# A hybrid decoder in split float32: modulation sums finished as columns, rotary products merged, evictions moved within their step

## The chip, the cores and the metric

The kernel runs on one core of one Trainium2 chip. The metric is the device time of one execution in microseconds (us); the kernel before takes 1912.27 us, the median of three runs (1906.89 to 1913.08). The engines are named as in the profile: PE (TensorE, matmuls), PEld (its weight loads), DVE (VectorE), ACT (ScalarE), POOL (GpSimd) and SP (SyncE, which here issues nearly all DMAs). Each engine works through its own instructions in a fixed order and waits at an instruction whose inputs, or whose buffer, aren't ready.

## The reference

Two layers are applied to 1024 positions of width 1024. Each has a token-mixing and a channel-mixing sub-layer, both normalised, both modulated by a vector `c`:

```python
mod = silu(c) @ ada_w[l] + ada_b[l]              # 6 x 1024
shift_m, scale_m, gate_m, shift_f, scale_f, gate_f = split(mod, 6)
h = rms_norm(x, g_pre_mix[l]) * (1 + scale_m) + shift_m
q, k, v, u = split(h @ w_in[l] + b_in[l])
q, k = partial_rotary(q), partial_rotary(k)      # first 16 of each head's 64
mix = concat(window_attention(q, k, v, sinks[l]), causal_pool(u)) @ w_out[l]
x = x + gate_m * rms_norm(mix, g_post_mix[l])
h = rms_norm(x, g_pre_ffn[l]) * (1 + scale_f) + shift_f
f = (silu(h @ w_gate[l]) * (h @ w_up[l])) @ w_down[l]
x = x + gate_f * rms_norm(f, g_post_ffn[l])
```

There are 8 query heads and 2 key heads, a window of 128, and an FFN of width 2816. All in float32.

## The kernel before

**Matmuls.** A float32 product is made of three matmuls on halves. `split` (L218) rounds a tile into a high part by a cast on ACT (L220) and takes the rest as a low part by a subtraction on DVE (L221); `mm3` (L262) issues high x high, low x high and high x low (L263, L266, L267) into one accumulator bank `acc`. Four such banks hold the four 128-row tiles of half the sequence (512 positions, `T`); each half is carried by itself. `msc` are banks for transposes and small products.

**Order.** The program is written as generators that yield at their steps. `run` (L682) advances a main stream and, by given ratios, side streams beside it; the instructions go into a scheduler that lays out each engine's order. So what is written ahead of a `yield`, or behind it, decides beside which main step it stands.

**A layer's stages.** `dense` (L1461) holds the projection of the pooled channels (`u_pass`, L754) and of queries and keys (`q_pass`, `kv_pass`), with attention on the first half beside it. `mix_out` (L1011) is the output projection, done by `natural_proj` (L653) in two halves of 512 columns (`nh`); for each, eight steps `k` add into the four banks, and behind the last one the banks are read: the squares' sum on ACT (`square_sum`, L501) and a product with the gate row `G` on DVE (L680). Attention on the second half runs beside it: `att_rotary` (L776) turns queries and keys in six DVE operations of 128x80 (L784 to L789), `att_keys` and `att_queries` split (L809, L832) and transpose them (L814, L835), the scores follow (L855, L856), then the softmax (L858 to L883) and its transposes (L893). The FFN's up products come in pairs of column blocks (`up_pair`, L1126): sums of weight blocks on DVE (L1166, L1167, L1171, L1172), each then split and multiplied in a product of 24 matmuls (T2, T3, T1, B22, T4), the banks combined on DVE (L1151). L1172 makes the operand of T3. The down products follow.

**The modulation** is a side stream. One sum (`ada_sum`, L285) covers 512 of the 6144 outputs: eight slices of `ada_w`, 128x512 each, are loaded into `ar` (two buffers) and added on DVE into one tile `ada`, scaled by `c` (L296 the first, L298 the rest). This leaves 128 partial sums a column, still to be added over the partitions. Three ways follow. For the FFN's shift and scale (`ada_pair`, L404) and for the gates (`ada_gate`, L457) the tile is split into two `ph` tiles and two matmuls with a picking vector `picks` add over the partitions to a row (L412, L413; L469, L470). `ada_pair` then gathers four rows and transposes them to columns (L420). A gate stays a row: bias and weight are loaded as rows into `ar` (L466, L467) and applied in two DVE operations of 1x512 (L471, L472), and the row is written to memory (L473), from where `load_gate` (L482) spreads it over the partitions as `G`. For the next layer's token-mixing (`ada_columns`, L435) four matmuls take 128 columns of `ada` each as weights and a column of ones as the moving operand, so the sums come out as columns at once (L441). `ada_stream` (L487) runs the sums one after another and closes each right behind its last step.

## Time and profile before

| | |
|---|---|
| median of 3 runs | 1912.27 us |
| the profiled execution's own time | 1915.26 us |
| its span | 1913.5 us |
| mean granted PE clock | 0.993 |
| busy: PE / DVE / ACT | 98% / 81% / 49% of the span |
| L298, the accumulations of the modulation | 140 times, 746 ns each, 104.5 us busy |
| L220 / L221, the splits | 388 times each, 868 / 986 ns |

The time runs slightly past the span, which begins with the first instruction that the profile shows. Start times in rows are from the span's start. The mean durations of L220 and L221 mix tiles of 128x512 and of 128x1024. In a row of a timeline "x4" stands for neighbouring instructions that were put together, and the bracket gives how long the engine was idle ahead of the row and whose end it waited for. The first layer takes about the first half of the span, the second the rest: its stages come some 940 us later.

### The profile page before, as it was taken

What the parts mean: (1) busy time and instruction counts of PE and PEld (TensorE: products, weight loads), DVE (VectorE), ACT (ScalarE), POOL (GpSimd) and SP (SyncE); (2) the same over time, 40 slices, a digit from 0 to 9 for tenths busy, and PEclk for the clock granted to TensorE, in tenths of its full rate; (3) what the DMA queues carried; (4) which work ended last, traced back from release to release, by engine and by line L of the source; (5) the groups of instructions that cost most, each with busy time, mean ns of one, the idle gap of its engine ahead of it and who ended that gap; (6) DMA issues with size and microseconds to landing.
All of it is one profiled execution on the core that took longest, in us unless ns stands there. A gap on an engine that the chain in (4) does not pass through costs nothing.

```text
span 1913.5 us, 26037 instructions
## 1 busy us (share of the span) xinstructions
PE 1866.0 (98%) x8954; PEld 1541.1 (81%) x8954; DVE 1541.9 (81%) x2913; ACT 946.4 (49%) x1786; POOL 20.4 (1%) x67
## 2 busy tenths in 40 slices
PE   7999999999999999999999989999999999999997
PEld 5887788888878788888888868888887887888886
DVE  7899886678788888788878988846888888877687
ACT  4875795553222223445548667845622222244452
POOL 0000000000000000000000000000000000000000
PEclk9999999999999999999999989999999999999999
DMA  9345563555555655944554464536754566574342
GB/s 343 108 144 161 160 220 127 187 182 192 183 180 187 206 206 172 320 144 149 175 175 138 125 179 165 177 110 211 218 181 149 197 211 201 198 251 150 114 152 102
DMA packets 229540, 341.86 MB, mean 179 GB/s; under 512 B 17016, under 2 KB 126472, under 8 KB 229408
## 3 DMA queue, kind: packets, MB, share of 16 engines
q1 hardware_dynamic: 228800, 338.10, 53.6%
q10 hardware_dynamic: 576, 2.10, 0.3%
q8 instruction: 70, 1.15, 0.2%
q14 instruction: 62, 0.51, 0.1%
q0 software_dynamic: 32, 0.00, 0.0%
HBM read 267.25 MB, written 72.89 MB: 178 GB/s over the span
## 4 chain that ended last, share of the span: by engine, by line
PE 77%; DVE 12%; DMA 5%; ACT 3%; issue 2%; SPq 0%; DVEq 0%; ACTq 0%; POOL 0%; POOLq 0%
PE acc L263 24%; PE acc L266 23%; PE acc L267 23%; DMA ar<-in_ada_w_dram 2%; DVE lo L221 2%; DMA raw<-in_w_up_dram 2%; DVE ada L298 1%; PE msc L893 1%; PE msc L561 1%; ACT hi L220 1%; DVE fn L1151 1%; PE pv L263 1%; PE pv L266 1%; ACT raw L554 1%; DMA ar<-x 1%
## 5 line engine op out<-in xcount | busy, mean ns | idle before, releaser
L220 ACT ACTIVATE hi<-raw 128x1024 fp32r<-128x1024 f32 (+1 forms) x388 | 331.9, 868 | 364.9 <-PE acc L266 198.8
L221 DVE TENSOR_TENSOR lo<-raw,hi 128x1024 fp32r<-128x1024 f32 (+1 forms) x388 | 379.9, 986 | 121.6 <-ACT hi L220 117.4
L263 PE MATMUL acc<-t,hi 128*128 128x512 f32 x704 | 275.1, 391 | 5.8 <-ACT hi L220 5.8
L266 PE MATMUL acc<-t,hi 128*128 128x512 f32 x704 | 274.7, 390 | 0.0
L267 PE MATMUL acc<-t,lo 128*128 128x512 f32 x704 | 272.1, 390 | 0.1
L263 PE MATMUL acc<-bh,hi 128*128 128x512 f32 x520 | 202.9, 390 | 0.0
L267 PE MATMUL acc<-bh,lo 128*128 128x512 f32 x520 | 202.4, 389 | 0.0
L263 PE MATMUL acc<-hT,hi 128*128 128x512 f32 x480 | 190.2, 396 | 0.6 <-DVE fn L680 0.6
L266 PE MATMUL acc<-hT,hi 128*128 128x512 f32 x480 | 188.4, 393 | 0.0
L267 PE MATMUL acc<-hT,lo 128*128 128x512 f32 x480 | 187.5, 391 | 0.0
L1151 DVE TENSOR_TENSOR fn<-acc,fn 128x512 f32<-128x512 f32 x220 | 150.3, 684 | 39.4 <-PE acc L267 39.1
L263 PEld LDWEIGHTS acc<-t,hi 128*128 128x128 f32 x704 | 132.4, 188 | 35.3 <-ACT hi L220 8.2
L267 PEld LDWEIGHTS acc<-t,lo 128*128 128x128 f32 x704 | 132.4, 188 | 29.3 <-DVE lo L221 1.5
L266 PEld LDWEIGHTS acc<-t,hi 128*128 128x128 f32 x704 | 132.5, 188 | 27.2
L266 PE MATMUL acc<-ph,hi 128*128 128x512 f32 x320 | 124.7, 390 | 0.0
L1087 ACT ACTIVATE fn<-fn 128x512 f32<-128x512 f32 x44 | 27.8, 633 | 185.7 <-DVE fn L1151 185.7
L298 DVE SCALAR_TENSOR_TENSOR ada<-ar,c_act,ada 128x512 f32<-128x512 f32 x140 | 104.5, 746 | 12.5 <-DMA ar<-in_ada_w_dram 11.3
L267 PEld LDWEIGHTS acc<-bh,lo 128*128 128x128 f32 x520 | 97.6, 188 | 20.4
L263 PEld LDWEIGHTS acc<-bh,hi 128*128 128x128 f32 x520 | 97.6, 188 | 20.2 <-ACT sb L1249 0.2
L263 PE MATMUL acc<-hi 128*128 128x512 f32 x256 | 103.6, 410 | 2.4 <-DVE fn L680 2.0
L263 PEld LDWEIGHTS acc<-hT,hi 128*128 128x128 f32 x480 | 90.2, 188 | 19.2 <-DVE fn L680 1.4
L267 PEld LDWEIGHTS acc<-hT,lo 128*128 128x128 f32 x480 | 90.1, 188 | 18.6 <-issue 0.2
(315 smaller groups left out, 3813.5 us busy)
## 6 DMA issues: line engine op xcount, KB each, us to landing
ar<-in_ada_w_dram SPq DMA_DIRECT2D x160, 256.0 KB
raw<-in_w_gate_dram SPq DMA_DIRECT2D x44, 512.0 KB
raw<-in_w_up_dram SPq DMA_DIRECT2D x44, 512.0 KB
raw<-in_w_in_dram SPq DMA_DIRECT2D x80, 256.0 KB
raw<-keeps SPq DMA_DIRECT2D x40, 512.0 KB
keeps<-fn SPq DMA_DIRECT2D x66, 256.0 KB
two_b<-in_w_down_dram SPq DMA_DIRECT2D x30, 512.0 KB
raw<-keepa SPq DMA_DIRECT2D x25, 512.0 KB
```

Source lines behind the costliest of these rows:

```text
L220: a = nc.scalar.activation(hi, src, AF.Copy)
L221: v = nc.vector.tensor_sub(lo, src, hi.bitcast(F32))
L263: ins = nc.tensor.matmul(dst, lh, rh, start=first, stop=False)
L266: nc.tensor.matmul(dst, lh, rl, start=False, stop=False)
L267: return nc.tensor.matmul(dst, ll, rh, start=False, stop=last)
L298: ins = nc.vector.scalar_tensor_tensor(acc, w, c_act[:, i : i + 1], acc, op0=ALU.mult, op1=ALU.add)
L554: nc.scalar.activation(hf, bank, AF.Identity, bias=shift, scale=scale)
L561: ins = nc.tensor.transpose(bank[:, t * P : (t + 1) * P], src[t], ident)
L893: nc.tensor.transpose(bank[:, i * P : (i + 1) * P], s[:, ii, ck * P : (ck + 1) * P], ident)
L1087: nc.scalar.activation(g, g, AF.Silu)
L1151: nc.vector.tensor_add(halves_of(dst)[m], bank, halves_of(src)[m])
```

## The change

**Sums as columns.** All sums now finish as `ada_columns` does: a helper `column_sums` issues the four matmuls with `ada` as weights. `ada_pair` is gone, and `ada_columns` serves the FFN's shift and scale. A gate is handled as a column too: bias and weight come from the transposed table `cols` (16 rows longer, from two more short loads a layer), two DVE operations of 128x4 replace those of 1x512, and the column is written to memory in elements of 4 bytes. The splits into `ph` and `picks` are gone for these sums.

**One step later.** `ada_stream` closes a sum only behind the first step of the next one.

**Rotary.** The tables of cosine and sine are doubled along a new axis, so that two products of 128x160 and two combinations of 128x80 replace the six operations; `vz` has four buffers instead of five.

**Evictions.** `natural_proj` reads each bank right behind its own last matmul, inside the last step, and `u_pass` its banks ahead of its last yield.

The core of the diff:

```diff
-    def ada_sum(l, n0, got, whole=False):
+    def ada_sum(l, n0, got):
...
-        if whole:
-            got.append(acc)
-        else:
-            got += [t_("ph", [P, 512], F32R), t_("ph", [P, 512], F32R)]
-            split(*got, acc)
+        got.append(acc)
         yield
...
+    def column_sums(acc):
+        bank = msc_bank()
+        for i in range(4):
+            nc.tensor.matmul(
+                bank[:, i : i + 1], acc[:, i * P : (i + 1) * P], ones[:, 0:1], start=True, stop=True
+            )
+        return bank[:, 0:4]
...
-        def close(half, hi, lo):
...
-            nc.sync.dma_start(gb, ada_b[l : l + 1, n0 : n0 + 512])
-            nc.sync.dma_start(gg, (g_post_ffn if sub else g_post_mix)[l : l + 1, o])
-            bank = msc_bank()
-            nc.tensor.matmul(bank[0:1, :], picks[:, 3:4], hi, start=True, stop=False)
-            nc.tensor.matmul(bank[0:1, :], picks[:, 3:4], lo, start=False, stop=True)
-            nc.vector.tensor_add(gb, bank[0:1, :], gb)
-            nc.vector.tensor_mul(gb, gb, gg)
-            nc.sync.dma_start(row[:, o], gb)
+        def close(half, acc):
+            bank = column_sums(acc)
...
+            nc.vector.tensor_add(gc, bank, cols[:, k0 : k0 + 4])
+            nc.vector.tensor_mul(gc, gc, cols[:, g0 : g0 + 4])
+            nc.sync.dma_start(row[0, half * 512 : half * 512 + 512].rearrange("(i p) -> p i", p=P), gc)
...
-        for l, n0, close, *whole in jobs:
+        ending = None
+        for l, n0, close in jobs:
             got = []
-            yield from ada_sum(l, n0, got, *whole)
-            close(*got)
+            for i, _ in enumerate(ada_sum(l, n0, got)):
+                yield
+                if ending and i == 0:
+                    ending()
+            ending = lambda close=close, got=got: close(*got)
+        yield
+        if ending:
+            ending()
...
                     mm3(banks[t], lh[:, tiles[t]], ll[:, tiles[t]], wh, wl, k == 0, k == K - 1)
+                    if k == K - 1:
+                        square_sum(ss, t, nh, banks[t])
+                        nc.vector.tensor_mul(fn[t][:, cs], banks[t], G[:, cs])
                 yield
-            for t in range(NT):
-                square_sum(ss, t, nh, banks[t])
-                nc.vector.tensor_mul(fn[t][:, cs], banks[t], G[:, cs])
...
-            yield
+            if k < KD - 1:
+                yield
         for g in range(4):
             ut = t_("uT", [P, UW])[:, : HALO + T]
...
             uts.append(ut)
+        yield
...
-        tmp = t_("rt", [P, 4, nr, RH])
-        nc.vector.tensor_mul(tmp[:, 0], t1, cb)
-        nc.vector.tensor_mul(tmp[:, 1], t2, sbc)
-        nc.vector.tensor_mul(tmp[:, 2], t2, cb)
-        nc.vector.tensor_mul(tmp[:, 3], t1, sbc)
-        nc.vector.tensor_sub(t1, tmp[:, 0], tmp[:, 1])
-        nc.vector.tensor_add(t2, tmp[:, 2], tmp[:, 3])
+        tmp = t_("rt", [P, 2, nr, ROT])
+        nc.vector.tensor_mul(tmp[:, 0], rot, cb)
+        nc.vector.tensor_mul(tmp[:, 1], rot, sbc)
+        for i in range(2):
+            a, b = slice(i * RH, (i + 1) * RH), slice((1 - i) * RH, (2 - i) * RH)
+            nc.vector.tensor_tensor(
+                out=rot[:, :, a], in0=tmp[:, 0, :, a], in1=tmp[:, 1, :, b], op=ALU.subtract if i == 0 else ALU.add
+            )
```

Three places in the engines' orders, before and after. The changed program has line numbers of its own: its L261, L264 and L265 are `mm3`, L788 and L809 the transposes of keys and queries (before L814, L835), L403 the column sum, L296 the accumulation (before L298), L650 the eviction (before L680).

The first is the border from `dense` to `mix_out` in the first layer, at 162 us of the trace. PE's order before:

```order
L267 MATMUL acc<-hi,uT 128x512
L412 MATMUL msc<-ph,picks 4x512
L413 MATMUL msc<-ph,picks 4x512
L814 MATMUL msc<-ident,hi 128x128 x4
L263 MATMUL acc<-hi 128x512 x3
L835 MATMUL msc<-ident,hi 128x128 x4
```

PE's order there in the changed kernel:

```order
L265 MATMUL acc<-hi,uT 128x512
L403 MATMUL msc<-ones_r,ada 128x1 x4
L788 MATMUL msc<-ident,hi 128x128 x4
L809 MATMUL msc<-ident,hi 128x128 x4
L261 MATMUL acc<-hi 128x512 x4
```

DVE's order at the same place in the changed kernel (`colp` are the finished columns, L757, L758 and L761 the rotary, L783 and L806 the splits that were L809 and L832):

```order
L296 SCALAR_TENSOR_TENSOR ada<-ar,c_act,ada 128x512
L758 TENSOR_TENSOR rt<-qkv,sin_t 128x160
L296 SCALAR_TENSOR_TENSOR ada<-ar,c_act,ada 128x512
L761 TENSOR_TENSOR qkv<-rt 128x10x8 x2
L415 TENSOR_TENSOR colp<-msc,cols 128x4
L775 TENSOR_TENSOR vz<-qkv,vz 128x64
L395 SCALAR_TENSOR_TENSOR colp<-colp,cols 128x4
L775 TENSOR_TENSOR vz<-qkv,vz 128x64
L757 TENSOR_TENSOR rt<-qkv,cos_t 128x160
L783 TENSOR_TENSOR hi<-qkv,hi 128x2x128
```

The column sum stands where the two picks stood, directly ahead of the keys' transposes, and on DVE the addition that reads it (L415) stands ahead of the split that those transposes read (L783).

The second is the border between the halves of `mix_out` in the second layer, at 1134 us. DVE's order before:

```order
L221 TENSOR_TENSOR ph<-msc,pth 128x512
L298 SCALAR_TENSOR_TENSOR ada<-ar,c_act,ada 128x512
L832 TENSOR_TENSOR hi<-qkv,hi 128x4x64
L680 TENSOR_TENSOR fn<-acc,G 128x512 x2
L298 SCALAR_TENSOR_TENSOR ada<-ar,c_act,ada 128x512
L680 TENSOR_TENSOR fn<-acc,G 128x512
L298 SCALAR_TENSOR_TENSOR ada<-ar,c_act,ada 128x512
L680 TENSOR_TENSOR fn<-acc,G 128x512
```

DVE's order there in the changed kernel (L832 is the softmax's masked maximum, L219 a split):

```order
L296 SCALAR_TENSOR_TENSOR ada<-ar,c_act,ada 128x512
L650 TENSOR_TENSOR fn<-acc,G 128x512
L415 TENSOR_TENSOR colp<-msc,cols 128x4
L650 TENSOR_TENSOR fn<-acc,G 128x512
L294 TENSOR_SCALAR ada<-ar,c_act 128x512
L832 ISA sb,st<-msc,mask 128x256
L832 ISA st 128x1
L832 ISA sb,st<-msc,mask 128x256
L832 ISA st 128x1
L219 TENSOR_TENSOR ph<-msc,pth 128x512
L296 SCALAR_TENSOR_TENSOR ada<-ar,c_act,ada 128x512
L650 TENSOR_TENSOR fn<-acc,G 128x512 x2
```

The first two evictions have moved ahead of the first accumulation of a new sum, the maxima and the split; the last two now stand behind them.

The third is the fifth pair of the FFN's products in the first layer, at 645 us. DVE's order before:

```order
L1088 TENSOR_TENSOR fn<-fn 128x512
L1172 TENSOR_TENSOR raw<-raw 128x8x128
L1196 TENSOR_TENSOR fn<-fn 128x512
L1151 TENSOR_TENSOR fn<-acc,fn 128x512
L221 TENSOR_TENSOR ph<-ada,ph 128x512
```

DVE's order there in the changed kernel (L1062, L1125, L1146 and L1170 are the former L1088, L1151, L1172 and L1196; `gc` is the gate's column):

```order
L1062 TENSOR_TENSOR fn<-fn 128x512
L1125 TENSOR_TENSOR fn<-acc,fn 128x512
L1170 TENSOR_TENSOR fn<-fn 128x512
L1146 TENSOR_TENSOR raw<-raw 128x8x128
L1125 TENSOR_TENSOR fn<-acc,fn 128x512
L435 TENSOR_TENSOR gc<-msc,cols 128x4
L436 TENSOR_TENSOR gc<-gc,cols 128x4
```

The sum of weight blocks (L1146) has gone behind an addition from the banks and a difference, and the gate's column comes out directly behind.

More of the change, by code (lines that the diff above doesn't have):

```diff
@@ L96, in hybrid_decoder_kernel @@
     dr = ctx.enter_context(tc.tile_pool(name="dr", bufs=1, space=DRAM))
-    SMALL = dict(junk=1, st=12, rs=8, ss=4, halo=8, rows=1, cols=2, colp=4, sk=2)
+    SMALL = dict(junk=1, gc=3, st=12, rs=8, ss=4, halo=8, rows=1, cols=2, colp=4, sk=2)
     SHARED = dict(hT=8, fn=4, raw=2, hi=3, lo=3, sa=2, sb=2, ar=2, ada=1, ph=3, G=1)
     REGIONS = dict(
-        mix=dict(cfa=2, cfb=2, qkv=5, bqkv=1, uT=4, pt=2, vz=5, rt=1, qT=1, pth=2, pwh=1, pwl=1),
+        mix=dict(cfa=2, cfb=2, qkv=5, bqkv=1, uT=4, pt=2, vz=4, rt=1, qT=1, pth=2, pwh=1, pwl=1),
         up=dict(t2=8, t1=8, t3=8, b22=8, t4=8),
@@ L147, in hybrid_decoder_kernel @@
     ones_r = const.tile([P, 1], F32R, name="ones_r")
-    picks = const.tile([P, 7], F32R, name="picks")
     c_raw = const.tile([P, KD], F32, name="c_raw")
@@ L450, in ada_columns @@
         return [
-            (l, (3 * sub + 1 - r // 2) * D + r % 2 * 512, lambda acc, r=r: close(r, acc), True)
+            (l, (3 * sub + 1 - r // 2) * D + r % 2 * 512, lambda acc, r=r: close(r, acc))
             for r in range(4)
```

79 lines of the change are left out of this document (23 added, 56 removed).

## Prediction

> **What bounds the kernel now.** I read the page's busy times first, then the waits of PE, then PE's rows around each long wait, and last the granted clock in windows of 3 us.
>
> ```profile
> PE 1866.0 (98%) x8954; PEld 1541.1 (81%) x8954; DVE 1541.9 (81%) x2913; ACT 946.4 (49%) x1786; POOL 20.4 (1%) x67
> ```
>
> ```profile
> PE msc L332 <- DVE ident L152: 11.1, 1, 11.1
> PE acc L263 <- ACT hi L220: 6.1, 5, 2.1
> PE msc L893 <- DVE sb L883: 3.8, 7, 0.9
> ```
>
> PE is the bound: work added to it costs its full length unless it falls into a wait, and work taken from another engine pays only where PE waits for it. The waits that the change can reach lie in the two mix stages. PE's timeline (start, duration, idle before it in brackets, and who ended the idle):
>
> ```profile
> 164.04 0.39 PE L412 MATMUL msc<-ph,picks 128*4 128x512 f32 x1 [1.76 <-ACT ph L220]
> 164.85 0.59 PE L413 MATMUL msc<-ph,picks 128*4 128x512 f32 x1 [0.43 <-DVE ph L221]
> 165.28 0.72 PE L814 MATMUL msc<-ident,hi 128*128 128x128 f32 x4
> ...
> 194.54 0.53 PE L835 MATMUL msc<-ident,hi 128*128 128x128 f32 x4 [1.41 <-DVE fn L680]
> ...
> 196.41 0.79 PE L263 MATMUL acc<-hi 128*128 128x512 f32 x1 [0.47 <-DVE fn L680]
> ...
> 1104.77 0.51 PE L814 MATMUL msc<-ident,hi 128*128 128x128 f32 x4 [1.67 <-DVE rt L787]
> 1105.55 0.97 PE L263 MATMUL acc<-hi 128*128 128x512 f32 x3 [0.27 <-ACT hi L220]
> ...
> 1134.75 0.51 PE L835 MATMUL msc<-ident,hi 128*128 128x128 f32 x4 [0.59 <-DVE hi L832]
> ...
> 1137.11 0.49 PE L263 MATMUL acc<-hi 128*128 128x512 f32 x1 [0.76 <-DVE fn L680]
> 1138.42 0.79 PE L263 MATMUL acc<-hi 128*128 128x512 f32 x1 [0.81 <-DVE fn L680]
> ```
>
> Idle: 2.19 us at 162, 1.88 at 193, 1.94 at 1103, 2.16 at 1134. Behind each the clock falls (columns: length, then busy us of PE, PEld, DVE, ACT, POOL, then the granted clock):
>
> ```profile
> 165.00:168.00 3.00, 3.00 (x13) 2.33 (x12) 3.00 (x11) 2.29 (x6) 0.00 (x0) 0.50 0.47 145
> 195.00:198.00 3.00, 2.53 (x9) 1.74 (x9) 3.00 (x6) 2.48 (x6) 0.00 (x0) 0.58 0.32 92
> ...
> 1107.00:1110.00 3.00, 3.00 (x9) 2.46 (x9) 2.96 (x5) 2.03 (x4) 0.00 (x0) 0.50 0.52 160
> ...
> 1137.00:1140.00 3.00, 2.08 (x4) 1.30 (x5) 2.84 (x8) 0.60 (x2) 0.00 (x0) 0.59 0.64 172
> 1140.00:1143.00 3.00, 3.00 (x8) 2.31 (x7) 2.95 (x11) 1.85 (x8) 0.14 (x1) 0.50 0.51 118
> 1475.00:1478.00 3.00, 1.79 (x8) 1.05 (x7) 3.00 (x5) 2.06 (x3) 0.00 (x0) 1.00 0.73 244
> ```
>
> At half clock for about 3.4 us PE loses about 1.7 us (twice that at 1137, where the low stretch covers most of two windows). A wait of 1.21 us (the 1475 window: 3.00 less 1.79 busy) left the clock at 1.00, so I take about 1.5 us idle within 3 us as the point where a fall begins. Idle and falls together cost 3.9, 3.6, 3.6 and 5.6 us at the four places: 16.7 us is all that is to be had there.
>
> The Trainium skill, "TensorE: Matmul & The Clock Gate", Part 1, puts the fall behind an idle window of about 3.4 us. No wait quoted here is that long, yet the rows show 0.50: the measurement decides. By that rule the falls would be no consequence of these waits and would stay when the waits shrink; the sum below would lose its two clock terms (4.3 us) and come out about 1916, inside the range of the forecast itself.
>
> **The change part by part.** *PE.* A sum that is a column already (L441) and a pair of picks (L469, L470):
>
> ```profile
> 790.69 0.95 PE L441 MATMUL msc<-ones_r,ada 128*128 128x1 f32 x8
> 791.50 0.49 PE L263 MATMUL acc<-bh,hi 128*128 128x512 f32 x1
> ...
> 649.88 0.40 PE L469 MATMUL msc<-ph,picks 128*1 128x512 f32 x1
> ...
> 650.35 0.43 PE L267 MATMUL acc<-t,lo 128*128 128x512 f32 x1
> ...
> 1150.05 0.41 PE L420 MATMUL msc<-ident,ar 4*128 4x4 f32 x4
> 1150.39 0.38 PE L855 MATMUL msc<-sa,qT 128*128 128x256 f32 x1
> ```
>
> Start to next start, a column sum holds PE for 0.81 us, a pair for 0.47: 16 x 0.34 = +5.4 us. The two groups of row transposes (L420, 0.34 each) go: -0.7. Four of the new sums (at 162, 197 and one in each layer's products) stand where PE waits anyway, -1.4. Net **+3.3**.
>
> *DVE and ACT.* Each of the 16 sums loses a cast and a subtraction of 128x512; the gates also swap two 1x512 operations for two of 128x4; the rotary goes from six operations to four. That is relief on an engine beside PE, worth only what it takes from PE's waits. I take **-1.0** of the waits for the softmax (L893, 3.8 us) and its like; bounds 0 and -3.8.
>
> *The border at 162.* DVE's rows:
>
> ```profile
> 162.57 0.75 DVE L298 SCALAR_TENSOR_TENSOR ada<-ar,c_act,ada 128x512 f32<-128x512 f32 x1 [0.36 <-DMA ar<-in_ada_w_dram]
> ...
> 164.72 0.42 DVE L809 TENSOR_TENSOR hi<-qkv,hi 128x256 fp32r<-128x256 f32 x1
> ```
>
> The column sum needs this L298 alone, which itself waited for its load: PE can start it at 163.3 instead of 164.04, and ends it at about 164.1. But the four transposes behind it need L809, and in the new order DVE waits for the column sum first (the addition to the columns), then has two copies, the scaling and a rotary product before L809: about 0.1 + 0.1 + 0.1 + 0.1 + 0.2 + 0.4 us from their rows' likes, so PE goes on at about 165.3, as before. The wait is cut in two, and so is what is gained: **0** (bounds -3.9 and +1).
>
> *The border at 193.* The four evictions (L680) move ahead of L809 and L832, but two L298 still stand among them, and PE now runs six attention matmuls and the first four of the next half before the transposes. By DVE's order the fourth bank comes free about 3 us after the last matmul, and the transposes wait for L809 and L832 behind it. **0** (bounds -3.6 and +2).
>
> *1103.* DVE's chain from the last of L738 to L809 is shorter by two rotary operations a block, some 0.4 us of the 1.67; the fall behind it goes with even odds. **-1.2** (bounds 0 and -3.6).
>
> *1134.* Here the evictions start before the stage's last matmuls end, and PE has eight transposes, six attention matmuls and four scores (some 2 us by the likes of their rows) before it asks for the third and fourth bank. Between the second and the third eviction, though, DVE has a sum, the softmax's maxima and a split:
>
> ```profile
> 1137.68 0.68 DVE L680 TENSOR_TENSOR fn<-acc,G 128x512 f32<-128x512 f32 x1
> ```
>
> The last eviction then ends some 3 us after the last matmul (an estimate: two evictions, the sum and a split of about 0.6 to 0.7 us each are left by then), and PE wants it at 2.5 to 3. I leave 1.0 us of idle, drop the fall, and round down: **-4.0** (bounds 0 and -5.6).
>
> *The FFN's products.* In each layer the two gate sums close one product step later. The third pair of column blocks then has on DVE, ahead of L1171 and L1172, the split of the gate slice, the gate's two small operations, L296 and one L298; in the fifth pair L1172 drops behind an eviction and L1196.
>
> ```profile
> 579.40 1.22 DVE L1166 TENSOR_TENSOR raw<-raw 128x1024 f32<-128x1024 f32 x1
> ...
> 588.27 1.21 DVE L1172 TENSOR_TENSOR raw<-raw 128x1024 f32<-128x1024 f32 x1
> ...
> 645.47 1.22 DVE L1172 TENSOR_TENSOR raw<-raw 128x1024 f32<-128x1024 f32 x1
> ```
>
> ```profile
> 646.38 0.39 PE L267 MATMUL acc<-t,lo 128*128 128x512 f32 x1
> 647.91 0.50 PE L263 MATMUL acc<-t,hi 128*128 128x512 f32 x1 [1.14 <-ACT hi L220]
> ```
>
> PE's product T3 waits for L1172 and the cast behind it. In the third pair L1172 ends at 589.48, and T3 begins (ten products of 24 steps of 0.227 us back from 646.77) at 592.2: with a cast of 1.1 us that leaves 1.6 us. The chain from L1166 to L1172 grows from 10.1 to about 13 us, but L1166 may start 1.4 us earlier, one place up: 0 to 1.4 us late. In the fifth pair 1.2 us comes on top of 1.14, of which the column sum fills 0.8. I take +0.8 a layer, **+1.6**; bounds 0 and +12.2 (below).
>
> *Queues and start.* The gate now goes out as 512 elements of 4 bytes, with the load of G right behind it on SP, and behind that the next weights:
>
> ```profile
> 1.27 5.45 DMA pos_i<-in_positions_dram
> ...
> 129.74 1.44 DMA gate<-ar
> ```
>
> ```profile
> 651.82 1.17 SPq L1134 DMA_DIRECT2D raw<-in_w_up_dram  x1
> ```
>
> ```profile
> 663.46 1.23 DVE L1166 TENSOR_TENSOR raw<-raw 128x1024 f32<-128x1024 f32 x1 [0.38 <-DMA raw<-in_w_up_dram]
> ```
>
> The row write took 1.44 us, the 4-byte read of the positions 5.45. These weights are issued 11.6 us before their first use, so up to some 4 us more of SP waiting is hidden: 0. The Trainium skill, "DMA: Bandwidth & Descriptors", Specifications, wants 512 B or more in a transfer, since shorter ones read, modify and write; it speaks against this write, and no run here shows such a write's price.
>
> ```profile
> 10.41 0.24 DVE cos_t L205
> ```
>
> At the start PE waits 11.1 us for the identity's cast behind these table operations; two rows more of them (0.2 each) and two short loads ahead of the first weights: **+0.5**, bounds 0 and +1.2.
>
> Sum: 3.3 - 1.0 + 0 + 0 - 1.2 - 4.0 + 1.6 + 0.5 = **-0.8 us** on the profiled execution's own 1915.26 us: 1914.5. That execution is 3.0 us above the median of the runs, so the forecast is **1911.5 us**.
>
> **The rivals.** *All four places empty* (DVE's relief puts it ahead everywhere): -16.7 for the -5.2 above, so 1911.5 - 11.5 = **1900 us**. For it: DVE is behind PE in each of the waits. Against: at 162 and 193 it waits for loads or has other work in front. *Slower: L1172 late in the products.* At the third pair 1.5 us of idle and a fall (3.2 us), at the fifth 1.2 us more and a fall (2.9), in two layers: 12.2 in place of 1.6, so about **1922 us**. It decides when L1172 in the third pair ends after 591.1 by today's times. For it: the same place in the first pair, with two L298 in front, shows PE's longest mid-run wait, 2.1 us. Against: DVE has slack ahead of L1166. *The change doesn't do what it says*: the evictions come early in the order but wait all the same, no mix wait shrinks, and the column sums' work stays: 3.3 + 1.6 + 0.5 = +5.4, so **1917.7 us**.
>
> **How the numbers follow.** A measurement of this kernel tells about 0.3% (5.7 us) from no change. Forecast 0.40 (1906 to 1917), all places empty 0.30, products late 0.16, only the added work 0.14, half of that beyond the bound. Faster 0.30, the same 0.47, slower 0.23. The range runs from the empty places (1899) to just below the full price of the late products (1921).
>
> **What would show it.** The columns' matmuls at 0.8 us a sum; PE's wait at 1134 under 1.2 us and the clock at 1.00 behind it; two waits instead of one at 162; PE's wait for ACT's cast in the third pair of products, absent today, under 1 us. I am wrong if the waits at 162 or 193 go (faster), or if the clock falls in the products where it does not today (slower).

## The result, and the profile after

The changed kernel takes **1942.62 us** (median of four, 1941.62 to 1946.39) against 1910.18 us of the kernel before in the same session (1906.89 to 1913.08): a ratio of 1.0174, interval 1.0150 to 1.0198. It is 32 us slower, beyond the range. The ratios here and below leave out two executions that were far slower than all others for a reason that isn't known, one of `e3_extra_small_writes` (2827 us) and one of the kernel before (6607 us).

The page of the changed kernel: busy times, and the line on DMA packets.

```profile
PE 1876.2 (97%) x9042; PEld 1556.2 (80%) x9042; DVE 1525.1 (79%) x2872; ACT 935.1 (48%) x1768; POOL 18.9 (1%) x67
...
DMA packets 233782, 341.86 MB, mean 176 GB/s; under 512 B 21249, under 2 KB 130737, under 8 KB 233649
```

The same line on packets of the kernel before:

```profile
DMA packets 229540, 341.86 MB, mean 179 GB/s; under 512 B 17016, under 2 KB 126472, under 8 KB 229408
```

DVE and ACT got the relief they were meant to get (1525 against 1542 us, 935 against 946). PE is busy 10.2 us longer, and the span of 1939.8 us leaves it idle for 63.6 us, where it was 47.5 before. There are 4,242 packets more, nearly all under 512 B: eight gate writes of 512 elements are 4,096 of them.

The waits of PE in the changed kernel (instruction, releaser: us in total, times, longest):

```profile
PE msc L867 <- DVE sb L857: 13.3, 7, 6.5
PE msc L327 <- DVE ident L151: 11.1, 1, 11.1
PE acc L261 <- ACT hi L218: 6.8, 5, 2.0
PE msc L867 <- DVE st L832: 4.4, 1, 4.4
```

The transposes of the softmax (L867, formerly L893) wait 17.7 us, where it was 3.8. What they wait for is DVE, and this is what DVE waits for, in the changed kernel:

```profile
DVE ada L296 <- DMA ar<-in_ada_w_dram: 32.0, 24, 6.4
DVE raw L1140 <- DMA raw<-in_w_up_dram: 25.6, 13, 6.6
```

and in the kernel before:

```profile
DVE raw L1166 <- DMA raw<-in_w_up_dram: 11.5, 7, 2.7
DVE ada L298 <- DMA ar<-in_ada_w_dram: 11.3, 18, 1.3
```

Loads that moved as many bytes as ever came late. The longest wait of PE shows why. SP's timeline of the changed kernel, in the mix of the second layer:

```profile
1080.04 0.68 SPq L437 DMA_DIRECT2D gate<-gc  x1
1080.83 0.45 SPq L304 DMA_DIRECT2D ar<-in_ada_w_dram  x1
...
1090.07 0.33 SPq L446 DMA_DIRECT2D G<-gate  x1
```

DVE's timeline there:

```profile
1083.91 0.70 DVE L965 TENSOR_TENSOR pt<-uT 128x527 f32<-128x527 f32 x1
1091.06 0.75 DVE L296 SCALAR_TENSOR_TENSOR ada<-ar,c_act,ada 128x512 f32<-128x512 f32 x1 [6.45 <-DMA ar<-in_ada_w_dram]
```

PE's timeline there:

```profile
1086.16 0.39 PE L261 MATMUL acc<-hi,hT 128*128 128x512 f32 x1
1093.05 0.45 PE L867 MATMUL msc<-ident,sb 128*128 128x128 f32 x1 [6.50 <-DVE sb L857]
```

And the windows (length, busy us of PE, PEld, DVE, ACT, POOL, then the granted clock, the share of time in which the DMA engines had work, and GB/s):

```profile
1082.00:1090.00 8.00, 4.54 (x25) 3.63 (x23) 2.54 (x6) 3.82 (x13) 0.00 (x0) 1.00 0.41 36
1090.00:1093.00 3.00, 0.00 (x0) 0.00 (x0) 1.94 (x9) 0.51 (x1) 0.00 (x0) 0.52 0.72 191
1093.00:1096.00 3.00, 2.95 (x9) 2.48 (x10) 2.01 (x5) 1.15 (x2) 0.00 (x0) 0.50 1.02 370
```

Read together: the gate (`gate<-gc`) goes out at 1080.04. For the next eight microseconds all DMA of the core moves 36 GB/s; then it recovers. The load of G, which needs the written gate, is issued only 10.0 us after it. The load of `ar` that SP issued 0.8 us behind the gate arrives when the gate is done, DVE stands 6.45 us before the one instruction that needs it, and the softmax, which needs nothing of it, stands behind that instruction in DVE's order. PE runs out of work for 6.50 us, and then runs at half clock. The other gates of the mix do the same: PE waits 3.81 us at 111.9 and 4.37 us at 1050.5. Not every new wait is theirs, though. One of 2.00 us in the products of the first layer, with a fall behind it, ends while the gate written at 652.97 has hardly left; it is taken up below:

```profile
653.30 0.79 PE L261 MATMUL acc<-t,hi 128*128 128x512 f32 x1 [2.00 <-ACT hi L218]
```

```profile
654.00:657.00 3.00, 3.00 (x9) 2.34 (x8) 2.78 (x3) 1.14 (x2) 0.00 (x0) 0.56 0.22 41
```

The places that the change was aimed at did improve. PE's rows of the changed kernel at the former 162, 193, 1103 and 1134:

```profile
169.81 0.51 PE L788 MATMUL msc<-ident,hi 128*128 128x128 f32 x4 [1.27 <-DVE hi L783]
...
196.98 1.15 PE L261 MATMUL acc<-hi 128*128 128x512 f32 x3 [0.72 <-ACT hi L640]
198.89 0.52 PE L261 MATMUL acc<-hi 128*128 128x512 f32 x1 [0.76 <-DVE fn L650]
...
1127.34 0.51 PE L788 MATMUL msc<-ident,hi 128*128 128x128 f32 x4 [1.37 <-DVE hi L783]
...
1157.05 0.38 PE L829 MATMUL msc<-sa,qT 128*128 128x256 f32 x1 [0.55 <-ACT qT L814]
...
1160.18 0.50 PE L264 MATMUL acc<-lo,hi 128*128 128x512 f32 x1 [1.06 <-DVE lo L219]
```

The windows behind them:

```profile
168.00:171.00 3.00, 1.73 (x15) 1.53 (x16) 2.41 (x12) 2.18 (x6) 0.00 (x0) 1.00 0.46 152
1129.00:1132.00 3.00, 3.00 (x17) 2.55 (x16) 3.00 (x6) 3.00 (x7) 0.00 (x0) 1.00 0.49 112
1162.00:1165.00 3.00, 3.00 (x15) 2.49 (x14) 2.87 (x10) 2.44 (x9) 0.32 (x1) 1.00 0.56 169
...
201.00:204.00 3.00, 3.00 (x12) 2.74 (x12) 1.88 (x7) 2.37 (x7) 0.00 (x0) 0.50 0.36 90
```

Three of the four falls of the clock are gone in this execution; the one at 193 is still there. The experiments say what that was worth.

### The profile page after: what moved, and what is told of

It reads as the page before. It is cut to its first block, busy times and chain, and to the rows that moved or that the text cites. A ratio compares the mean times of both kernels' runs of the same rounds, so it can differ in the third digit from the quotient of the medians.

```text
span 1939.8 us, 26118 instructions
## 1 busy us (share of the span) xinstructions
PE 1876.2 (97%) x9042; PEld 1556.2 (80%) x9042; DVE 1525.1 (79%) x2872; ACT 935.1 (48%) x1768; POOL 18.9 (1%) x67
## 4 chain that ended last, share of the span: by engine, by line
PE 72%; DVE 13%; DMA 9%; ACT 4%; issue 2%; SPq 0%; DVEq 0%; ACTq 0%; POOL 0%; POOLq 0%
PE acc L261 22%; PE acc L265 22%; PE acc L264 22%; DMA raw<-in_w_up_dram 4%; DMA ar<-in_ada_w_dram 3%; DVE lo L219 2%; PE msc L867 1%; DVE fn L1125 1%; ACT hi L218 1%; DVE ada L296 1%; DMA ar<-x 1%; PE msc L532 1%; PE msc L403 1%; PE pv L261 1%; PE pv L264 1%
## 5 line engine op out<-in xcount | busy, mean ns | idle before, releaser
L219 DVE TENSOR_TENSOR lo<-raw,hi 128x1024 fp32r<-128x1024 f32 (+1 forms) x388 | 380.4, 986 | 120.6 <-ACT hi L218 118.3
L261 PE MATMUL acc<-t,hi 128*128 128x512 f32 x704 | 277.1, 394 | 6.9 <-ACT hi L218 6.8
L265 PE MATMUL acc<-t,lo 128*128 128x512 f32 x704 | 274.4, 393 | 3.3 <-DVE lo L219 3.1
L264 PE MATMUL acc<-t,hi 128*128 128x512 f32 x704 | 275.9, 392 | 0.0
L261 PE MATMUL acc<-bh,hi 128*128 128x512 f32 x520 | 202.9, 390 | 0.0
L265 PE MATMUL acc<-bh,lo 128*128 128x512 f32 x520 | 202.5, 389 | 0.0
L261 PE MATMUL acc<-hT,hi 128*128 128x512 f32 x480 | 190.7, 397 | 2.6 <-ACT uT L738 2.0
L264 PE MATMUL acc<-hT,hi 128*128 128x512 f32 x480 | 188.2, 392 | 0.0
L265 PE MATMUL acc<-hT,lo 128*128 128x512 f32 x480 | 187.8, 392 | 0.0
L1125 DVE TENSOR_TENSOR fn<-acc,fn 128x512 f32<-128x512 f32 x220 | 150.2, 683 | 40.5 <-PE acc L265 40.4
L261 PEld LDWEIGHTS acc<-t,hi 128*128 128x128 f32 x704 | 133.4, 190 | 36.5 <-ACT hi L218 9.4
L265 PEld LDWEIGHTS acc<-t,lo 128*128 128x128 f32 x704 | 133.0, 189 | 33.3 <-DVE lo L219 5.5
L264 PEld LDWEIGHTS acc<-t,hi 128*128 128x128 f32 x704 | 133.4, 189 | 27.7
L296 DVE SCALAR_TENSOR_TENSOR ada<-ar,c_act,ada 128x512 f32<-128x512 f32 x140 | 104.5, 747 | 32.8 <-DMA ar<-in_ada_w_dram 32.0
L264 PE MATMUL acc<-ph,hi 128*128 128x512 f32 x320 | 124.7, 390 | 0.0
L265 PEld LDWEIGHTS acc<-bh,lo 128*128 128x128 f32 x520 | 97.6, 188 | 20.3
L261 PEld LDWEIGHTS acc<-bh,hi 128*128 128x128 f32 x520 | 97.7, 188 | 20.0
L261 PEld LDWEIGHTS acc<-hT,hi 128*128 128x128 f32 x480 | 90.4, 188 | 21.0 <-ACT uT L738 2.4
L265 PEld LDWEIGHTS acc<-hT,lo 128*128 128x128 f32 x480 | 90.1, 188 | 18.5
L264 PEld LDWEIGHTS acc<-hT,hi 128*128 128x128 f32 x480 | 90.4, 188 | 16.4
```

The lines of the kernel that those rows point to most:

```text
L219: v = nc.vector.tensor_sub(lo, src, hi.bitcast(F32))
L261: ins = nc.tensor.matmul(dst, lh, rh, start=first, stop=False)
L264: nc.tensor.matmul(dst, lh, rl, start=False, stop=False)
L265: return nc.tensor.matmul(dst, ll, rh, start=False, stop=last)
L296: ins = nc.vector.scalar_tensor_tensor(acc, w, c_act[:, i : i + 1], acc, op0=ALU.mult, op1=ALU.add)
L1125: nc.vector.tensor_add(halves_of(dst)[m], bank, halves_of(src)[m])
```

## The experiments

Every kernel below was timed against the kernel before on the same chip; the medians of that one were between 1908.6 and 1910.2 us. A ratio stands with its 95% interval.

### Is it the gate, and which part of it?

The changed kernel with the gate turned back into a row on PE and written as a row (`e1_row_write`):

```diff
-            nc.sync.dma_start(row[0, half * 512 : half * 512 + 512].rearrange("(i p) -> p i", p=P), gc)
+            turned = msc_bank()
+            nc.tensor.transpose(turned[0:4, 0:P], gc, ident)
+            gr = t_("rows", [P, P])[0:4]
+            nc.vector.tensor_copy(gr, turned[0:4, 0:P])
+            nc.sync.dma_start(row[0, half * 512 : half * 512 + 512].rearrange("(i p) -> i p", p=P), gr)
```

> The changed kernel, but each gate column (128x4) is turned to 4x128 by a PE transpose and copied by DVE, so that it is written in four pieces of 512 B instead of 512 elements of 4 B. Theory S (the small writes clog the memory side for some 10 us, the next load for the modulation lands late, DVE waits for it and PE behind DVE): the three waits of 3.8, 4.4 and 6.5 us go, with the clock falls behind them; 1905 to 1916 us. Theory O (the loss is the order: sums closed a step later, accumulations ahead of the softmax on DVE): 1935 to 1946 us. Theory Q (the loads only stand behind the small writes in SP's own queue): as S.

The changed kernel with the gate closed as before, by a split and picks, and the other sums as columns (`e2_old_gate`):

```diff
-            bank = column_sums(acc)
...
+            split(hi, lo, acc)
...
+            nc.tensor.matmul(bank[0:1, :], picks[:, 3:4], hi, start=True, stop=False)
+            nc.tensor.matmul(bank[0:1, :], picks[:, 3:4], lo, start=False, stop=True)
...
+            nc.sync.dma_start(row[:, o], gb)
```

> The changed kernel with the gates finished as before (split, two picks, a row of 1x512, a write in one piece of 2 KB), still one step later; the FFN's shift and scale stay columns. Theory S: 1905 to 1916 us, near e1_row_write. Theory O: 1930 us or more, since order and late close stay. Theory Q: as S.

The kernel before, with a second write of 512 elements of 4 bytes beside each gate's (`e3_extra_small_writes`):

```diff
             nc.sync.dma_start(row[:, o], gb)
+            extra = dr.tile([1, 512], F32, tag="extra", name="extra", bufs=4 * DEPTH)
+            nc.sync.dma_start(extra[0].rearrange("(i p) -> p i", p=P), c_act[:, 0:4])
```

> The kernel before, with one extra write of 512 elements of 4 B (a constant tile of 128x4, to memory that nobody reads) behind each of the eight gate writes. Theory S: slower by 15 to 30 us (1925 to 1940). Theory O: within 3 us of before. Theory Q: as S, since the loads stand behind the extra writes in the same queue.

The changed kernel with the gate on ACT's queue (`e4_other_queue`):

```diff
-            nc.sync.dma_start(row[0, half * 512 : half * 512 + 512].rearrange("(i p) -> p i", p=P), gc)
+            nc.scalar.dma_start(row[0, half * 512 : half * 512 + 512].rearrange("(i p) -> p i", p=P), gc)
```

> The changed kernel, with the gate's small writes issued by ACT on its own queue instead of SP's. Theory S: the loads are as late as in the changed kernel, 1935 to 1946 us. Theory Q: the loads no longer stand behind the writes, 1908 to 1920 us. Theory O: 1935 to 1946 us.

| kernel | median us | ratio to before |
|---|---|---|
| changed | 1942.62 | 1.0174 (1.0150 to 1.0198) |
| e1_row_write | 1917.22 | 1.0045 (1.0027 to 1.0064) |
| e2_old_gate | 1921.09 | 1.0052 (1.0032 to 1.0071) |
| e3_extra_small_writes | 1931.66 | 1.0113 (1.0087 to 1.0139) |
| e4_other_queue | 1947.11 | 1.0197 (1.0178 to 1.0216) |

e1 does all that the change does, and a transposition more for each gate, and only its write is another: 25.4 us of the 32 are gone. (DVE's order changes a little with it; `e16_gate_in_16_bytes` below is free of that.) e2, whose gates are closed as before, loses 21.5 of the 32. Both stay above the 1905 to 1916 us that were expected: some 7 to 11 us of the loss have another cause. The waits of DVE for the same two loads fall as well; in e1:

```profile
DVE ada L296 <- DMA ar<-in_ada_w_dram: 17.4, 18, 2.7
...
DVE raw L1144 <- DMA raw<-in_w_up_dram: 13.1, 11, 2.3
```

The window of e1 behind the gate that cost most above, and that of e4:

```profile
1070.00:1078.00 8.00, 7.60 (x47) 6.41 (x45) 6.01 (x18) 5.48 (x14) 0.00 (x0) 1.00 0.88 277
```

```profile
1085.00:1093.00 8.00, 4.86 (x26) 3.85 (x25) 2.60 (x8) 3.58 (x13) 0.00 (x0) 1.00 0.55 82
```

e4 says that it isn't SP's queue that holds the later loads up: from another queue the write costs as much. So the theory of a queue's order falls, and what is slow is the write and, with it, all other transfers.

e3 missed its place. Its extra writes read data that is ready at the start, so the scheduler sent all eight off between 57.9 and 73 us, instead of one beside each gate. It still shows the loss, and plainly: apart from the extra writes, every engine runs the same instructions in the same order as in the kernel before. DVE waits there for a short load, and PE behind it waits 16.6 us at one transposition, where it was 0.6:

```profile
DVE sk L1354 <- DMA sk<-in_sinks_dram: 15.9, 1, 15.9
```

### What of the write is it?

The kernel before with extra writes that copy the finished gate row, so that each must stay where the gate is written. They go to memory that nobody reads, and differ in form alone. As 512 elements of 4 bytes, 8 bytes apart (`e9_small_writes_in_place`), and as 128 elements of 16 bytes, 32 bytes apart (`e10_16_byte_writes`):

```diff
             nc.sync.dma_start(row[:, o], gb)
+            extra = dr.tile([512, 2], F32, tag="extra", name="extra", bufs=4 * DEPTH)
+            nc.sync.dma_start(extra[:, 0:1].rearrange("e a -> a e"), gb)
```

```diff
             nc.sync.dma_start(row[:, o], gb)
+            extra = dr.tile([1, 128, 8], F32, tag="extra", name="extra", bufs=4 * DEPTH)
+            nc.sync.dma_start(extra[:, :, 0:4], gb.rearrange("a (e f) -> a e f", f=4))
```

> The kernel before, and behind each gate write the same row a second time in 512 elements of 4 B (8 B apart, to memory that nobody reads); it depends on the gate, so that it stays at the gate's place. Theory S (512 small writes hold up the loads behind them by some 10 us): slower by 15 to 30 us, DVE waiting for the modulation's loads behind three or four of the eight. If the loss were the wait of G for the gate, or the changed order: within 4 us of before.

> As e9_small_writes_in_place, but the extra copy goes in 128 elements of 16 B. Theory S in its form 'each element costs the same': a quarter of that run's loss, 4 to 8 us. If the bytes counted, or any short write were as bad: as that run, 15 to 30 us.

Then 128 elements of 4 bytes, 8 bytes apart (`e13_128_of_4_bytes`), four times the write of e10 (`e14_512_of_16_bytes`), and 512 elements of 4 bytes, 512 bytes apart (`e15_4_bytes_far_apart`):

```diff
+            extra = dr.tile([512, 2], F32, tag="extra", name="extra", bufs=4 * DEPTH)
+            nc.sync.dma_start(extra[0:128, 0:1].rearrange("e a -> a e"), gb[:, 0:128])
```

```diff
+            for c4 in range(4):
+                extra = dr.tile([1, 128, 8], F32, tag="extra", name="extra", bufs=16 * DEPTH)
+                nc.sync.dma_start(extra[:, :, 0:4], gb.rearrange("a (e f) -> a e f", f=4))
```

```diff
+            extra = dr.tile([512, 128], F32, tag="extra", name="extra", bufs=4 * DEPTH)
+            nc.sync.dma_start(extra[:, 0:1].rearrange("e a -> a e"), gb)
```

> The kernel before, with an extra write of 128 elements of 4 B behind each gate write (e9_small_writes_in_place had 512, +42 us; e10_16_byte_writes 128 of 16 B, no loss). If the element's size decides: a loss of some 5 to 15 us. If only the number decides: none, like e10, within 3 us of before.

> The kernel before, with 512 extra elements of 16 B behind each gate write, in four transfers of 128. If the element's size decides: within 4 us of before (three more issues on SP included). If the number decides: 20 to 45 us slower, like e9.

> As e9_small_writes_in_place, but the 512 elements of 4 B lie 512 B apart instead of 8 B. If neighbours in one block of memory make the writes slow: much of the 42 us goes, under 1925 us. If every 4 B write is slow by itself: 1940 to 1955 us.

And the changed kernel with its gate columns taken with a stride of 4, so that each partition holds four neighbours and writes them as one element of 16 bytes, with no turn back into a row (`e16_gate_in_16_bytes`):

```diff
+            by = acc.rearrange("p (q i) -> p i q", i=4)
...
+                nc.tensor.matmul(bank[:, i : i + 1], by[:, i, :], ones[:, 0:1], start=True, stop=True)
...
+            nc.sync.dma_start(row[0, o].rearrange("(p i) -> p i", i=4), gc[:, 0:4])
```

> The changed kernel, with the gate's columns taken with a stride of four, so that each partition holds four neighbouring outputs: bias and weight are loaded, and the gate is written, in 128 elements of 16 B; no transpose. By theory S with the size deciding: 1912 to 1919 us, as e1_row_write or a little better (no transposes, but two loads more a gate). If short writes of any size hurt: 1925 us or more.

The table gives, beside the ratio, what all DMA of the core moved from 1.5 to 9.5 us after each of the eight writes, by the windows of each trace:

| kernel | the write | ratio | GB/s, eight writes in order |
|---|---|---|---|
| before | row | 1 | 260, 196, 292, 332, 219, 188, 302, 338 |
| changed | 512 x 4 B, adjacent | 1.0174 | 52, 43, 56, 11, 51, 45, 60, 11 |
| e9 | + 512 x 4 B, 8 B apart | 1.0213 (1.0198 to 1.0228) | 114, 119, 125, 144, 120, 107, 131, 131 |
| e13 | + 128 x 4 B, 8 B apart | 1.0191 (1.0169 to 1.0213) | 139, 137, 174, 178, 163, 135, 169, 158 |
| e15 | + 512 x 4 B, 512 B apart | 1.0064 (1.0047 to 1.0081) | 230, 186, 267, 282, 198, 187, 281, 278 |
| e10 | + 128 x 16 B, 32 B apart | 0.9996 (0.9987 to 1.0006) | 236, 169, 268, 248, 203, 181, 247, 257 |
| e16 | 128 x 16 B, adjacent | 1.0055 (1.0039 to 1.0071) | 204, 111, 228, 193, 163, 240, 229, 216 |

In the windows, the share in which the DMA engines had work (the last number but one) tells a slow transfer from a missing one. The window behind the sixth write in the kernel before, then in e9, then in e13:

```profile
1060.45:1068.45 8.00, 8.00 (x49) 6.56 (x48) 7.79 (x24) 5.49 (x13) 0.00 (x0) 1.00 0.61 188
```

```profile
1082.26:1090.26 8.00, 8.00 (x51) 6.76 (x50) 3.83 (x12) 4.48 (x9) 0.00 (x0) 1.00 0.58 107
```

```profile
1080.57:1088.57 8.00, 8.00 (x50) 6.62 (x49) 5.12 (x18) 4.52 (x10) 0.00 (x0) 1.00 0.68 135
```

At this write the engines had work for about as long as before, and moved 43% and 28% less. At other writes the share falls too. But GB/s divided by that share tells the kernels apart at all eight: 288 to 349 before, 278 to 315 in e10, 312 to 344 in e15 and 264 to 337 in e16, but 170 to 240 in e9, 163 to 247 in e13 and 35 to 159 in the changed kernel. So:

- A kernel with an extra write of small elements that nobody waits for is 37 to 42 us slower (e13 and e9, more than was expected of either). It isn't the wait for the gate itself.
- Not the number of elements alone: with 128 of 4 bytes the transfers are as slow as with 512, and 128 of 16 bytes cost nothing.
- Not that the elements are short alone: at 16 bytes there is no loss, and with 512 elements of 4 bytes set 512 bytes apart the transfers kept their pace (186 to 282 GB/s).
- What the bad cases share is elements of 4 bytes close beside each other. What in the memory's path makes that slow, these runs can't show. Size and spacing are not wholly apart either: a stretch of 32 bytes takes 8 elements in the changed kernel, 4 in e9 and e13, 2 in e16 and 1 in e10 and e15.

There is a rival to all of this: an edit also lets the scheduler lay out the engines' orders anew. The traces, laid beside each other instruction by instruction, settle it for two pairs. In e9 and e15 all five engines run the same instructions in the same order, so the 28 us between them (1.0213 against 1.0064) come from the distance of the elements alone. e16 has the orders of the changed kernel, but for the gate's own operands and 16 short loads more on SP, so its 22 us come from the elements' form. The order of e9 and e15 isn't that of the kernel before: on DVE it differs in more than a hundred places, in e10 in some thirty, and e13 has an order of its own. So some of the 42 and 37 us can be the order's, and for e13 no price of the elements alone can be given.

e14 costs too, 1940.38 us, 1.0157 (1.0142 to 1.0172), but for another reason. Its window behind the seventh write, and then SP's rows at the third:

```profile
1497.68:1505.68 8.00, 8.00 (x37) 6.63 (x36) 5.00 (x7) 1.26 (x2) 0.00 (x0) 1.00 0.22 58
```

```profile
542.95 2.46 SPq L476 DMA_DIRECT2D extra<-ar  x4
549.95 0.35 SPq L1157 DMA_DIRECT2D keepa<-sb  x1
550.34 0.44 SPq L306 DMA_DIRECT2D ar<-in_ada_w_dram  x1
550.88 0.41 SPq L1137 DMA_DIRECT2D raw<-in_w_gate_dram  x1
```

SP in e10 at the same place:

```profile
541.75 0.37 SPq L1136 DMA_DIRECT2D raw<-in_w_gate_dram  x1
```

Here the engines have work for 22% of the time only: the loss is of another kind, as hardly anything was issued. With three more issues the scheduler put the next weights behind a store that waits for DVE, 9.1 us later than in e10 (5.3 when the two executions, which are 3.84 us apart there, are laid over each other). So e14 gives no price of 512 elements of 16 bytes.

e15 is 12 us slower although its transfers keep their pace. Where that comes from wasn't found. The changed order is a candidate; its profiled execution, 1915.14 us, was the fastest of four, so its trace shows little of it.

e16 takes the small elements out of the changed kernel, and 22 us go: 1920.48 us, a little above the 1912 to 1919 expected. It isn't better than e1.

### What were the other parts worth?

The kernel before with the evictions and the merged rotary, and no columns (`e5_no_columns`); with the evictions alone (`e6_evictions_only`); and e1 with the evictions put back (`e7_evictions_back`). The edit of e6, which e5 has too and e7 takes out of e1:

```diff
+                    if k == K - 1:
+                        square_sum(ss, t, nh, banks[t])
+                        nc.vector.tensor_mul(fn[t][:, cs], banks[t], G[:, cs])
                 yield
-            for t in range(NT):
-                square_sum(ss, t, nh, banks[t])
-                nc.vector.tensor_mul(fn[t][:, cs], banks[t], G[:, cs])
...
-            yield
+            if k < KD - 1:
+                yield
```

> The kernel before, with the merged rotary and the moved evictions, and with nothing of the sums' change. What is left of the loss when the gates are written in long pieces is about 8 us. Theory W (that rest is the column sums' own matmuls, some 6.5 us of PE): this kernel has none of it, 1900 to 1910 us, at or below before. Theory E (the rest comes from the evictions' move): 1914 to 1920 us. Theory L (it comes from closing a sum one step later): as W.

> The kernel before, with the evictions moved and nothing else. Theory W: 1902 to 1911 us. Theory E: 1913 to 1920 us. Theory L: as W.

> The changed kernel with the gates written in long pieces (as e1_row_write) and the evictions back behind the step. Theory W: 1914 to 1924 us. Theory E: 1905 to 1912 us. Theory L: as W.

e5 took 1909.82 us, 1.0007 (0.9997 to 1.0017), e6 1910.02 us, 1.0007 (0.9997 to 1.0017), e7 1915.73 us, 1.0040 (1.0025 to 1.0055) against e1's 1.0045. Neither the evictions nor the rotary bring anything that can be measured. In the traces of e5 and e6 two of the four falls are still there, at 193 and at 1134 (e5: a clock of 0.71 from 195 to 198 us and of 0.61 from 1136 to 1139), and PE's waits at 1134 add up to 1.58 and 1.85 us, where it was 2.16. So the moved evictions by themselves don't do what the sum priced there at -4.0.

e1 with each sum closed at once again (`e8_close_at_once`), and e5 with the late close but the sums split as before (`e11_late_close_old_sums`):

```diff
-        ending = None
         for l, n0, close in jobs:
             got = []
-            for i, _ in enumerate(ada_sum(l, n0, got)):
-                yield
-                if ending and i == 0:
-                    ending()
-            ending = lambda close=close, got=got: close(*got)
...
+            yield from ada_sum(l, n0, got)
+            close(*got)
```

> The changed kernel with the gates written in long pieces (as e1_row_write) and every sum closed right behind its last step. Theory W: 1913 to 1922 us, since the column sums stay. Theory E: the same. Theory L: 1905 to 1911 us.

> The kernel before with the merged rotary, the moved evictions and the close one step later, but with the sums split and picked as before (e5_no_columns plus the late close). Theory W (the rest of about 8 us is the column sums' matmuls): 1903 to 1912 us. If the late close cost it: 1914 to 1920 us.

e8 took 1921.66 us, 1.0066 (1.0051 to 1.0081), and e11 1916.64 us, 1.0036 (1.0023 to 1.0049). The two effects don't add: columns, with the gates turned back into rows, cost 11 us on top of an immediate close (e8 over e5) and 2 us, less than the intervals, on top of a late close (e1 over e11); the late close by itself costs 5.5 us (e11 over e5). What makes the late close cost with split sums wasn't traced.

The kernel before with 16 column sums more, beside the splits, whose results nobody reads (`e12_extra_column_sums`):

```diff
             split(*got, acc)
+            bank = msc_bank()
+            for i in range(4):
+                nc.tensor.matmul(
+                    bank[:, i : i + 1], acc[:, i * P : (i + 1) * P], ones[:, 0:1], start=True, stop=True
+                )
```

> The kernel before, with the four column matmuls issued beside each of the 16 split sums as well, their result unread. It prices a column sum by itself: 16 x 0.81 us = 13 us on PE if nothing hides them, so 1919 to 1923 us by theory W; under 1914 us if they fall into PE's waits.

1923.91 us, 1.0078 (1.0063 to 1.0093): 15 us for 16 sums, 0.94 us each. The group of their instructions in e12's costliest lines of PE (two passes to a matmul, so 128):

```profile
L316 PE MATMUL msc<-ones_r,ada 128*128 128x1 f32 x128 | 15.8, 245 | 1.0 <-DVE rt L792 0.7 <-DVE ada L298 0.2
```

## Why the prediction was wrong

**The step that failed is "Queues and start".** It priced the gate's write at most like the one transfer of 4-byte elements that the trace held, the read of the positions (5.45 us, 4 us more than the row write), and took those 4 us to be hidden, because the FFN's raw weights are issued 11.6 us before their first use. Both halves failed. The write holds for some ten microseconds (`G<-gate` is issued 10.0 us after `gate<-gc`; it was 1.5 us with the row of the kernel before, and is 2.9 us in e1), and a read was no measure of it. And the slack was misread. In the kernel before the weights issued at 651.82 leave ahead of the gate's write. Those behind it are issued at 657.69 and land 5.70 us later, and it is for them that L1166 at 663.46 already waits 0.38 us: there was no slack. SP's rows, and the load in the chain of work that ended last:

```profile
654.31 0.25 SPq L473 DMA_DIRECT2D gate<-ar  x1
...
657.69 0.51 SPq L1134 DMA_DIRECT2D raw<-in_w_up_dram  x1
```

```profile
657.69 5.70 DMA raw<-in_w_up_dram
```

And the cost isn't the write's own: while it lasts, every other load crawls, and in the mix the ones with no slack are the loads of `ar` right behind it, which DVE takes in order ahead of the softmax. I had named what was behind the gate on its queue, and had not asked what else was in flight. In place of 0 the term is 22 to 25 us (changed against e16 and e1). For the 25.4 us to e1, the two traces show 16.5 us more of PE's idle time and 7.9 us more of its busy time, at a mean clock of 0.989 against 0.995 (spans 1939.8 and 1915.4, busy 1876.2 and 1868.3).

The Trainium skill, "DMA: Bandwidth & Descriptors", Specifications, which the prediction set beside this step, says that transfers below 512 B miss line rate, as they read, modify and write. It was right in direction: this write was a bad one. Whether a read-modify-write is behind it no run here shows, and by size alone the runs don't bear the rule out: e10's elements of 16 bytes cost nothing (0.9996), and e15's of 4 bytes leave the other transfers their pace.

**The gains: a second error, of size.** The four places were priced at 16.7 us to be had, and 5.2 of it was taken, from one execution with four falls of the clock. That execution took 1915.26 us against medians of 1908.6 to 1910.2. e10 has nearly the waits of the kernel before, its profiled execution took 1908.37 us, and of the four falls only those at 193 and 1134 are in it. PE in e10:

```profile
162.89 0.39 PE L412 MATMUL msc<-ph,picks 128*4 128x512 f32 x1 [1.66 <-ACT ph L220]
163.71 0.40 PE L413 MATMUL msc<-ph,picks 128*4 128x512 f32 x1 [0.42 <-DVE ph L221]
...
1470.60 0.50 PE L263 MATMUL acc<-t,hi 128*128 128x512 f32 x1 [2.11 <-ACT hi L220]
```

The windows behind these two places in e10:

```profile
165.00:168.00 3.00, 2.58 (x15) 1.94 (x14) 3.00 (x8) 3.00 (x7) 0.00 (x0) 1.00 0.60 160
1471.00:1474.00 3.00, 3.00 (x15) 2.02 (x14) 3.00 (x5) 1.45 (x2) 0.00 (x0) 1.00 0.22 84
```

2.08 and 2.11 us of idle, and the clock stays at 1.00; 2.19 us at the first of these places cost the kernel before a fall. So the point of "about 1.5 us idle within 3 us" is no threshold: the same wait is followed by a fall in one execution and by none in another. The granted clock tells more. In each execution the falls lie on one grid of 3.41 us: in the kernel before they begin, up to its end, at 164.76, 195.48, 536.81, 1106.84 and 1137.56, whole numbers of such steps apart, and last one step or two. There the wait at 162 lay in one step (161.35 to 164.76, PE idle for 2.09 us of it). In e10 the border between two steps, at 162.98, cut it in two, and the steps beside it hold 1.66 and 0.65 us of idle time. So one execution's falls are no measure of what the median pays. The Trainium skill, "TensorE: Matmul & The Clock Gate", Part 1, says that the window in which activity is judged, about 3.4 us, runs freely, so that the phase matters; the two traces agree with that. That a whole window has to be idle they don't bear out, as falls follow steps with about 2 us of idle time.

What a fall that goes is worth these runs don't show. Three went in the changed kernel, where the gate's write covers it; e5 and e6 gain nothing, but keep the two that e10 has.

By the other steps:

- *Column sums* (+5.4 of PE work): nearly right. e12 prices a sum at 0.94 us where 0.81 was read; with a pair of picks at the 0.47 read from before, 16 sums bring 16 x 0.47 = 7.5. That is about the 8.6 us that e1 is slower, but e8 and e11 show that the close has a part in it, so the 8.6 can't be divided further.
- *The softmax's waits* (-1.0): right without the gate's write. In e1 they are 2.9 us in place of 3.8:

```profile
PE msc L871 <- DVE sb L861: 2.9, 5, 1.3
```

- *162* (0): one wait of 1.27 us in place of two of 2.19 together, a little better. *193* (0): right, 1.48 us and a fall. *1103* (-1.2): right in kind, 1.37 us where it was 1.94, no fall. *1134* (-4.0): as written, waits of 0.55 and 1.06 us, clock 1.00. None of it shows as a gain in the median.
- *The FFN's products* (+1.6): the rival "L1172 late in the products" came true in one of its four places. In the changed kernel PE waits 2.00 us for ACT's cast in the fifth pair of the first layer, where it was 1.14, and the clock falls behind it (0.56), which was named as a sign of being wrong; the rows stand in the section on the result. In the third pair there is no wait in either layer, and in the fifth pair of the second it is 0.98 where it was 1.32. In e1 the wait of the first layer, 1.97 us, stands before the gate's transposition instead, with a fall as well, and PE waits for ACT's casts less than the 6.1 us of before:

```profile
PE acc L261 <- ACT hi L218: 1.9, 2, 1.2
```

- *Start* (+0.5): 0; the wait is 11.1 us in both.

None of the rivals was the mechanism of the 32 us. Without the write the forecast would still have been off: -0.8 us against the 8.6 us that e1 is slower. The gains of 5.2 are part of that; the late close, 5.5 us in e11, had a term only in the products and the places named above. Where those 5.5 us arise stays open.

## What to carry to other kernels

A write to memory is priced by what it does to the transfers around it, not by its own length: look at what the DMA moves in the microseconds behind it, and at which load with no slack is in flight then. A value that lies as columns is cheaper turned into a row on PE first, or laid out so that each partition writes some neighbours as one element (25 and 22 us here). Before a wait is called hidden, find the very load that the first use waits for. Before a gain is read from falls of the clock, look whether another execution of the same kernel has them. And when an experiment adds a transfer, compare the engines' orders as well as the times.

## What the runs showed of the hardware

- Eight writes of 512 elements of 4 bytes, each starting 4 or 8 bytes from the next, cost 22 to 28 us where the engines' orders are the same (changed against e16, e9 against e15). In the 8 us behind such a write the whole core moves 11 to 60 GB/s (4 bytes apart) or 107 to 144 (8 bytes apart), where it was 188 to 338; 128 elements 8 bytes apart leave 135 to 178 (e13). Another queue makes no difference (e4). Elements of 16 bytes, 128 to a write, cost nothing (e10).
- The share in which the DMA engines have work can miss such a stall (0.61 before, 0.58 in e9, behind the sixth write); GB/s divided by it does not (308 and 184).
- Waits of 2.1 to 2.2 us on PE were followed by half clock in one execution and by full clock in another. The falls lie on a grid of 3.41 us, and it matters whether a wait lies in one step of it.
